# Regrouping the small matmuls of a gated recurrence and of windowed attention inside a two-layer mixer kernel

## The chip, the cores and the metric

The kernel runs on one core of one Trainium2 chip. The metric is the device time of one execution in microseconds. A core has five engines that run side by side and wait for one another through semaphores: TensorE (PE in the profile, its weight loads shown apart as PEld), VectorE (DVE), ScalarE (ACT), GpSimd (POOL, nearly unused here) and SyncE (SP), which issues most of the DMAs.

## What is computed

Two layers (DEPTH = 2) of one mixer run over 640 tokens of width 2048: 128 context tokens and 512 latent ones. In each layer a normalised and modulated x is multiplied by one input matrix of 6656 columns, whose columns feed three branches side by side; their outputs are concatenated, multiplied by one output matrix, gated and added to x. The two branches that the change touches are these (cut from the reference):

```
def sink_attend(qb, keys, vals, mask, sink):          # 8 query heads, 2 kv heads, blocks of 128 queries
    s = jnp.einsum('bhgqd,bhkd->bhgqk', qb, keys) * (HEAD_DIM ** -0.5)
    ...
    p = jnp.exp(s - m)
    denom = jnp.sum(p, axis=-1, keepdims=True) + jnp.exp(sk - m)
    out = jnp.einsum('bhgqk,bhkd->bhgqd', p / denom, vals)

def hgrn_scan(q, k, v, logf, s0):                     # 4 heads, both directions, chunks of 32 tokens
    def step(S, xs):
        b = jnp.cumsum(lfc, axis=-2)
        qe = qc * jnp.exp(b)
        ke = kc * jnp.exp(-b)
        att = jnp.where(causal, jnp.einsum('bhtd,bhsd->bhts', qe, ke), 0.0)
        o = jnp.einsum('bhtd,bhdv->bhtv', qe, S) + jnp.einsum('bhts,bhsv->bhtv', att, vc)
        S = jnp.exp(b_last)[..., 0, :, None] * S + jnp.einsum('bhsd,bhsv->bhdv', kc * jnp.exp(b_last - b), vc)
```

## The kernel before

**The big products.** Tokens stand as five tiles of 128. Each weight tile of 256 KB is loaded by SP (`wraw`, L662), split into a rounded part `wh` on ACT (L670) and a remainder `wl` on DVE (L671), and each product is made of three matmuls (`wh` with the rounded activations `hh`, `wl` with `hh`, `wh` with the remainder `hl`). `rowmajor` gives 512 columns for five token tiles (L682, L683, L684, 128x512 each); `colmajor` gives 128 columns for all tokens (L690, a 128x384 and a 128x256 matmul for each of the three). All of this work runs through `self.pm`, five PSUM banks named m.

**The small work.** Attention, the recurrence and the gating branch are generators in a list, `self.side`. `rowmajor` and `colmajor` call `tick()` every few matmuls, which runs the first generator to its next `yield`; so small instructions are written down between big ones. They use three PSUM banks named s (`bank()`). A further generator, `ada_gen`, computes modulation vectors on DVE from weights that SP loads (L311, `aacc<-wa,s,aacc`).

**What sets the order.** The program is recorded through a scheduling layer. It keeps data dependencies, and from the written order and its own idea of times it lays down a fixed sequence for each engine. At run time each engine works through its sequence strictly in order, and an instruction whose inputs are late holds up all that stands behind it on that engine. `keep_in_program_order(x)` adds one rule: x may not be placed ahead of the instruction that was written before it on its engine. It does not forbid that others are placed between.

**Attention** (`attn`, 20 calls: two layers, two kv heads, one context tile t = 0 and four latent tiles). The scores of four heads are made, masked and exponentiated on ACT (L955); DVE forms the reciprocal of the denominator (L958); ACT multiplies each head's row by it (L960, four ACTIVATEs). Then for each block of 128 keys: four transposes through TensorE, one per head, into one s bank (L971); ACT copies the bank into a rounded part (L974), DVE forms the remainder (L975), and three 128x512 matmuls add into the output bank: L983 with the rounded part, L984 with the remainder, L985 with the rounded part again. There are 56 such latent key blocks, and four for the context tile.

**The recurrence** (`hgrn`, 8 calls: two layers, four heads). After the states are made, the five token tiles are gone through as steps n. In a step `build(n)` writes the decayed keys of each direction d into a buffer `K[d]` of which there is one (7 ACT copies per direction, L1120 and L1124). Four matmuls per direction with 32 output columns each (L1138) give a 128x128 block of scores in a bank of its own; DVE masks it into `att[d]` (L1141), and adds both directions (L1143). One step later TensorE transposes the sum (L1161), ACT copies it (L1163, `aT`), and two steps after that three matmuls (L1150, two L1153) give the tile's output, which ACT squares and copies (L1156, L1157).

## Times and profile before

| | us |
|---|---|
| median of 3 runs | 2282.91 (2281.86 to 2283.32) |
| the profiled execution | 2287.63 |
| its span, first to last instruction | 2285.8 |
| PE busy in the span | 2242.6 (13259 matmuls) |
| DVE / ACT busy | 1381.1 / 943.9 |
| transposes L971 | 240, 45.6 busy |
| score matmuls L1138 | 640 records, 33.7 busy |

The profile shows one execution. Busy times of PE overlap, since the next matmul starts while the one before drains; what a matmul costs is therefore read from the distance between starts. A matmul on unrounded 32-bit numbers stands in the trace as two records, so 320 matmuls of L1138 are 640 records. In a timeline row the columns are the start in us, the length in us, engine, line, operation, output and inputs, shapes, the number of merged instructions, and in brackets the idle time of the engine before them with what ended it. PEld rows are weight loads; one that had to wait shows idle time there even where PE itself still drains older work.

### The profile page before, as it was taken

The numbers are of one execution on the slowest core, as the hardware profiler recorded it, in microseconds if no ns is written. First come the engines' busy times: TensorE is split into PE (matmuls) and PEld (weight loads), VectorE is DVE, ScalarE is ACT, GpSimd is POOL, SyncE is SP. The second block draws the span as 40 slices with busy tenths as digits, with TensorE's granted clock in tenths as the row PEclk, the third lists the DMA queues.
The fourth block names the chain that finished last, engine by engine and source line by source line (L and its number), as shares of the span: only waits on it lengthen the run. The fifth ranks groups of instructions, "written<-read, shape, count | busy, mean of one in ns | idle before, by whom it ended". The sixth has DMA issues, their size and how long they took to land.

```text
span 2285.8 us, 35095 instructions
## 1 busy us (share of the span) xinstructions
PE 2242.6 (98%) x13259; PEld 1945.6 (85%) x13259; DVE 1381.1 (60%) x2666; ACT 943.9 (41%) x2306; POOL 0.7 (0%) x8
## 2 busy tenths in 40 slices
PE   7999999999999999999989999999999999999999
PEld 4766778999999998978877887799999999898887
DVE  4457967748577575776668555844846644264332
ACT  3423355445464562422223345543635545233111
POOL 0000000000000000000000000000000000000000
PEclk9999999999999999999999999999999999999999
DMA  9776533324334254465553321422423322326332
GB/s 354 243 258 209 171 95 117 117 78 145 103 114 133 83 154 129 144 224 182 177 181 94 101 61 48 131 60 82 140 76 103 111 69 82 94 70 205 113 106 79
DMA packets 265550, 299.03 MB, mean 131 GB/s; under 512 B 16771, under 2 KB 166165, under 8 KB 263845
## 3 DMA queue, kind: packets, MB, share of 16 engines
q1 hardware_dynamic: 252656, 270.09, 37.9%
q10 hardware_dynamic: 12724, 26.71, 3.7%
q8 instruction: 104, 1.70, 0.3%
q14 instruction: 66, 0.53, 0.1%
HBM read 281.69 MB, written 15.04 MB: 130 GB/s over the span
## 4 chain that ended last, share of the span: by engine, by line
PE 87%; DVE 6%; DMA 5%; ACT 1%; issue 1%; ACTq 0%; SPq 0%; DVEq 0%
PE m L690 36%; PE m L682 12%; PE m L684 12%; PE m L683 12%; DMA wa<-in_w_ada_dram 4%; DVE aacc L311 2%; PE s L249 2%; PE s L925 2%; PE s L971 1%; PE s L1138 1%; DVE wl L671 1%; PE s L983 1%; PE s L690 1%; PE s L984 1%; PE s L1153 1%
## 5 line engine op out<-in xcount | busy, mean ns | idle before, releaser
L671 DVE TENSOR_TENSOR wl<-wr,wh 128x512 fp32r<-128x512 f32 (+1 forms) x535 | 366.5, 687 | 547.5 <-ACT wh L670 546.5
L670 ACT ACTIVATE wh<-wr 128x512 fp32r<-128x512 f32 (+1 forms) x535 | 335.9, 629 | 870.6 <-PE m L684 501.7
L683 PE MATMUL m<-wl,hh 128*128 128x512 f32 x1440 | 568.1, 395 | 5.9 <-DVE wl L671 5.7
L682 PE MATMUL m<-wh,hh 128*128 128x512 f32 x1440 | 571.0, 397 | 1.6 <-ACT hh L396 1.5
L684 PE MATMUL m<-wh,hl 128*128 128x512 f32 x1440 | 566.1, 393 | 0.0
L690 PE MATMUL m<-hh,wh 128*128 128x384 f32 x2016 | 479.1, 317 | 0.2 <-DVE ev L1189 0.2
L690 PE MATMUL m<-hh,wl 128*128 128x384 f32 x2016 | 468.1, 311 | 0.0
L690 PE MATMUL m<-hl,wh 128*128 128x384 f32 x2016 | 467.3, 311 | 0.0
L311 DVE SCALAR_TENSOR_TENSOR aacc<-wa,s,aacc 128x512 f32<-128x512 f32 x480 | 344.1, 746 | 84.9 <-DMA wa<-in_w_ada_dram 82.7
L682 PEld LDWEIGHTS m<-wh,hh 128*128 128x128 f32 x1440 | 271.9, 189 | 73.8 <-issue 9.8
L683 PEld LDWEIGHTS m<-wl,hh 128*128 128x128 f32 x1440 | 272.0, 189 | 65.7 <-DVE wl L671 9.6
L690 PEld LDWEIGHTS m<-hh,wh 128*128 128x128 f32 x2016 | 310.8, 189 | 14.7 <-issue 9.3
L684 PEld LDWEIGHTS m<-wh,hl 128*128 128x128 f32 x1440 | 271.8, 189 | 58.5 <-issue 2.4
L690 PEld LDWEIGHTS m<-hh,wl 128*128 128x128 f32 x2016 | 311.5, 189 | 2.0 <-issue 1.8
L690 PEld LDWEIGHTS m<-hl,wh 128*128 128x128 f32 x2016 | 311.2, 189 | 2.0 <-issue 1.4
L1124 ACT ACTIVATE mg<-ev,Dt 128x32 f32<-128x32 f32 x480 | 113.3, 309 | 10.3 <-PE s L1138 10.1
L955 ACT ACTIVATE g<-g,st,qs 128x384 f32<-128x384 f32 (+1 forms) x64 | 48.1, 752 | 31.6 <-DVE st L951 31.6
L975 DVE TENSOR_TENSOR g<-s,g 128x512 fp32r<-128x512 f32 x56 | 38.6, 690 | 36.3 <-ACT g L974 29.2
L971 PE MATMUL s<-misc,g 128*128 128x128 f32 x240 | 45.6, 284 | 5.9 <-ACT g L960 5.1
L960 ACT ACTIVATE g<-g,st 128x384 f32<-128x384 f32 (+2 forms) x80 | 43.9, 605 | 13.3 <-DVE st L958 13.3
L925 PE MATMUL s<-kT,g 128*128 128x256 f32 (+1 forms) x288 | 47.3, 305 | 0.0
L971 PEld LDWEIGHTS s<-misc,g 128*128 128x128 f32 x240 | 29.6, 142 | 20.1 <-ACT g L960 12.3
(278 smaller groups left out, 1832.4 us busy)
## 6 DMA issues: line engine op xcount, KB each, us to landing
wr<-in_w_in_dram SPq DMA_DIRECT2D x406, 256.0 KB, 2.9
wa<-in_w_ada_dram SPq DMA_DIRECT2D x296, 256.0 KB, 2.9
wr<-in_w_out_dram SPq DMA_DIRECT2D x128, 256.0 KB, 3.0
wa<-in_w_ada_dram SPq DMA_DIRECT2D x16, 1024.0 KB, 7.0
wa<-in_w_in_dram SPq DMA_DIRECT2D x9, 1024.0 KB, 6.4
mg<-in_w_ada_dram SPq DMA_DIRECT2D x4, 1280.0 KB
x<-mg SPq DMA_DIRECT2D x20, 256.0 KB, 2.6
mg<-x ACTq DMA_DIRECT2D x5, 1024.0 KB, 6.1
```

The source lines that it names most:

```text
L249: return self.nc.tensor.matmul(acc[32 * q:32 * q + 32, 0:n], lhsT=lhs[:, kk, :], rhs=rhs, start=kk < 4, stop=kk >= 12, skip_group_check=True)
L311: nc.vector.scalar_tensor_tensor(acc[:, cd], r, sc, acc[:, cd], op0=ALU.mult, op1=ALU.add)
L670: nc.scalar.activation(wh, raw, AF.Copy)
L671: nc.vector.tensor_tensor(wl, raw, wh.bitcast(F32), op=ALU.subtract)
L682: nc.tensor.matmul(ps, lhsT=hh, rhs=wh[:, 0], start=k == 0, stop=False)
L683: nc.tensor.matmul(ps, lhsT=hh, rhs=wl[:, 0], start=False, stop=False)
L684: nc.tensor.matmul(ps, lhsT=hl, rhs=wh[:, 0], start=False, stop=k == KT - 1)
L690: self.nc.tensor.matmul(ps[hf][:, 0:n], lhsT=w[:, a], rhs=h[:, o:o + n], start=k == 0 and i == 0, stop=k == KT - 1 and i == 2)
L925: nc.tensor.matmul(so, lhsT=x[:, hs], rhs=y[:, ks], start=i == 0, stop=i == 2, skip_group_check=True)
L955: nc.scalar.activation(dst[h], src[h], AF.Exp, bias=nmx[:, h:h + 1], scale=rq[:, h:h + 1], accum_out=den[:, h:h + 1])
L971: nc.tensor.transpose(pb[:, h * P:(h + 1) * P], dst[h][:, kb * P:(kb + 1) * P], self.ident)
L1124: nc.scalar.activation(blk[:, 4 * i + q], e[:, q], AF.Copy, scale=dd[:, i, c:c + 1])
```

## The change

Four things are edited, and nothing of the arithmetic but one order of addition.

- In `attn`, the scaling by the reciprocal denominator is shared: heads 0 and 2 go to DVE (`tensor_scalar`), heads 1 and 3 stay on ACT.
- In the same function the loop over key blocks first writes the three value matmuls of the block before, and then the four transposes of this block. The value matmul with the remainder comes first of the three. The transposes go from head 3 down to head 0. The instructions of such a group, all but its first, are tied with `keep_in_program_order`.
- In `hgrn`, both directions' scores go into one bank, and are masked by one DVE operation of 256 columns; for that `att` becomes one tile of two halves, and the mask constant swaps its halves.
- In a step n of `hgrn` these are now written in one row and tied: the eight score matmuls of tile n, the transpose of tile n-1, and the three output matmuls of tile n-2. Transpose and output share one bank `y`. The copies on DVE and ACT and `build(n + 1)` are written behind them. A head has seven steps with two yields each (before: eight steps and 13 yields).

```
--- before.py
+++ after.py
@@ -69,7 +69,7 @@
     for cd in range(2):
         misc[cd::32, 248 + cd] = 1.0
     c["misc"] = misc
-    c["tri"] = np.stack([q <= k, q >= k], axis=1).astype(np.float32)
+    c["tri"] = np.stack([q >= k, q <= k], axis=1).astype(np.float32)
     return c
 
 
@@ -218,11 +218,11 @@
             mf = self.g(512)
             nc.scalar.dma_start(mf, C["mask"][:, 512 * i:512 * i + 512])
             nc.vector.tensor_copy(self.mask[:, 512 * i:512 * i + 512], mf)
-        self.att = [cst.tile([P, P], F32, name=f"att{d}") for d in range(2)]
+        self.att = cst.tile([P, 2, P], F32, name="att")
         self.tp = [cst.tile([P, 5, 5], F32, name=f"tp{i}") for i in range(2)]
         for d in range(2):
             nc.gpsimd.memset(self.tp[d], 0.0)
-            nc.gpsimd.memset(self.att[d], 0.0)
+            nc.gpsimd.memset(self.att[:, d], 0.0)
         self.snk = cst.tile([P, 2, 8], F32, name="snk")
         self.nsnk = cst.tile([P, 2, 8], F32, name="nsnk")
         nc.scalar.dma_start(self.snk, I["attn_sink"].partition_broadcast(P))
@@ -957,18 +957,33 @@
         nc.vector.tensor_tensor(den, den, es, op=ALU.add)
         nc.vector.reciprocal(den, den)
         for h in range(4):
-            nc.scalar.activation(dst[h], dst[h], AF.Copy, scale=den[:, h:h + 1])
+            if h % 2:
+                nc.scalar.activation(dst[h], dst[h], AF.Copy, scale=den[:, h:h + 1])
+            else:
+                nc.vector.tensor_scalar(dst[h], dst[h], den[:, h:h + 1], None, op0=ALU.mult)
         yield
         yield
         yield
         yield
         o = self.bank()
         pend = None
+        keep = self.tc.keep_in_program_order
         for kb in range(nb + 1):
+            if kb > 0:
+                first, last = kb == 1, kb == nb
+                if t > 0:
+                    v = [self.vT[:, gi, i, vb[kb - 1]] for i in range(2)]
+                    nc.tensor.matmul(o, lhsT=v[0], rhs=pend[1], start=first, stop=False)
+                    keep(nc.tensor.matmul(o, lhsT=v[0], rhs=pend[0], start=False, stop=False))
+                    keep(nc.tensor.matmul(o, lhsT=v[1], rhs=pend[0], start=False, stop=last))
+                else:
+                    nc.tensor.matmul(o, lhsT=self.vprm(gi), rhs=pend, start=first, stop=last)
             if kb < nb:
                 pb = self.bank()
-                for h in range(4):
-                    nc.tensor.transpose(pb[:, h * P:(h + 1) * P], dst[h][:, kb * P:(kb + 1) * P], self.ident)
+                for h in range(3, -1, -1):
+                    x = nc.tensor.transpose(pb[:, h * P:(h + 1) * P], dst[h][:, kb * P:(kb + 1) * P], self.ident)
+                    if kb or h < 3:
+                        keep(x)
                 if t > 0:
                     pt = (self.g(512, F32R), self.g(512, F32R))
                     nc.scalar.activation(pt[0], pb, AF.Copy)
@@ -976,15 +991,6 @@
                 else:
                     pt = self.g(512)
                     nc.scalar.activation(pt, pb, AF.Copy)
-            if kb > 0:
-                first, last = kb == 1, kb == nb
-                if t > 0:
-                    v = [self.vT[:, gi, i, vb[kb - 1]] for i in range(2)]
-                    nc.tensor.matmul(o, lhsT=v[0], rhs=pend[0], start=first, stop=False)
-                    nc.tensor.matmul(o, lhsT=v[0], rhs=pend[1], start=False, stop=False)
-                    nc.tensor.matmul(o, lhsT=v[1], rhs=pend[0], start=False, stop=last)
-                else:
-                    nc.tensor.matmul(o, lhsT=self.vprm(gi), rhs=pend, start=first, stop=last)
             pend = pt
             yield
         nc.scalar.activation(A, o, AF.Copy)
@@ -1128,41 +1134,55 @@
         K = build(0)
         yield
         aTs, sums = {}, {}
-        for n in range(NT + 3):
+        both = lambda a: a.rearrange("p d k -> p (d k)")
+        keep = self.tc.keep_in_program_order
+        for n in range(NT + 2):
             if n < NT:
+                ab = self.bank()
                 for d in range(2):
                     qe = pre[d][1]
-                    ab = self.bank()
                     for i in range(4):
                         ri = 3 - i if d else i
-                        nc.tensor.matmul(ab[32 * i:32 * i + 32, 0:P], lhsT=qe[:, n * P + 32 * i:n * P + 32 * i + 32],
+                        x = nc.tensor.matmul(ab[32 * i:32 * i + 32, d * P:(d + 1) * P],
+                                         lhsT=qe[:, n * P + 32 * i:n * P + 32 * i + 32],
                                          rhs=K[d][:, ri * P:(ri + 1) * P], start=True, stop=True,
                                          skip_group_check=True)
-                    nc.vector.copy_predicated(self.att[d], self.m8[:, 1 - d], ab[:, 0:P])
-                asum = self.sml.tile([P, P], F32, tag="asum", name=self.nm("asum"), bufs=2)
-                nc.vector.tensor_tensor(asum, self.att[0], self.att[1], op=ALU.add)
-                sums[n] = asum
-                if n + 1 < NT:
-                    K = build(n + 1)
-            if n >= 3:
-                j = n - 3
-                oo = self.bank()
-                nc.tensor.matmul(oo[:, 0:P], lhsT=aTs[j], rhs=vj[j], start=True, stop=j == 0)
+                        if d or i:
+                            keep(x)
+            if n > 0:
+                y = self.bank()
+            if 1 <= n <= NT:
+                x = nc.tensor.transpose(y[:, 0:P], sums.pop(n - 1), self.ident)
+                if n < NT:
+                    keep(x)
+            if n >= 2:
+                j = n - 2
+                oo = y[:, P:2 * P]
+                x = nc.tensor.matmul(oo, lhsT=aTs[j], rhs=vj[j], start=True, stop=j == 0, skip_group_check=True)
+                if n <= NT:
+                    keep(x)
                 if j > 0:
                     for d in range(2):
-                        nc.tensor.matmul(oo[:, 0:P], lhsT=pre[d][2][:, j * P:(j + 1) * P],
-                                         rhs=S[d][:, order[d].index(j) - 1], start=False, stop=d == 1)
+                        keep(nc.tensor.matmul(oo, lhsT=pre[d][2][:, j * P:(j + 1) * P],
+                                              rhs=S[d][:, order[d].index(j) - 1], start=False, stop=d == 1,
+                                              skip_group_check=True))
+            if n < NT:
+                nc.vector.copy_predicated(both(self.att), both(self.m8), ab[:, 0:2 * P])
+                asum = self.sml.tile([P, P], F32, tag="asum", name=self.nm("asum"), bufs=2)
+                nc.vector.tensor_tensor(asum, self.att[:, 0], self.att[:, 1], op=ALU.add)
+                sums[n] = asum
+            if 1 <= n <= NT:
+                aT = self.sml.tile([P, P], F32, tag="aT", name=self.nm("aT"), bufs=2)
+                nc.scalar.activation(aT, y[:, 0:P], AF.Copy)
+                aTs[n - 1] = aT
+            if n >= 2:
                 junk = self.sml.tile([P, P], BF16, tag="junk", name=self.nm("junk"), bufs=1)
-                nc.scalar.activation(junk, oo[:, 0:P], AF.Square, accum_out=ss[:, j:j + 1])
-                nc.scalar.activation(ob[:, j * P:(j + 1) * P], oo[:, 0:P], AF.Copy)
+                nc.scalar.activation(junk, oo, AF.Square, accum_out=ss[:, j:j + 1])
+                nc.scalar.activation(ob[:, j * P:(j + 1) * P], oo, AF.Copy)
+            if n + 1 < NT:
+                K = build(n + 1)
             yield
-            if 1 <= n <= NT:
-                tb = self.bank()
-                nc.tensor.transpose(tb[:, 0:P], sums.pop(n - 1), self.ident)
-                aT = self.sml.tile([P, P], F32, tag="aT", name=self.nm("aT"), bufs=2)
-                nc.scalar.activation(aT, tb[:, 0:P], AF.Copy)
-                aTs[n - 1] = aT
-                yield
+            yield
         nc.scalar.activation(ss, ss, AF.Ln, bias=self.bias[:, 0:1], scale=1.0 / P)
         nc.scalar.activation(ss, ss, AF.Exp, scale=-0.5)
         for j in range(NT):
```

**What this moves on TensorE in the recurrence.** First the place in layer 0, head 0, at step 1 of 5, before the change. L1138 are the score matmuls of one direction (`g_4966` forward, `g_5158` backward), L1161 the transpose; L690 are big column products.

```order
L1138 MATMUL s_5444<-mg_4962,g_4966 32x128 x4
L690 MATMUL m_5300<-hh_688,wh_5434 128x384
...
L690 MATMUL m_5300<-hl_718,wh_5434 128x384
L1138 MATMUL s_5450<-mg_4962,g_5158 32x128 x4
L690 MATMUL m_5301<-hl_718,wh_5434 128x256
L690 MATMUL m_5300<-hh_717,wl_5432 128x384
L690 MATMUL m_5301<-hh_717,wl_5432 128x256
L1161 MATMUL s_5484<-misc,asum_5406 128x128
```

The same place after the change; L1146 are the score matmuls, L1155 the transpose, L1161 now the first output matmul.

```order
L690 MATMUL m_5300<-hh_717,wl_5432 128x256
L1146 MATMUL s_5453<-mg_4961,g_4965 32x128 x4
L1146 MATMUL s_5453<-mg_4961,g_5157 32x128 x4
L1155 MATMUL s_5462<-misc,asum_5403 128x128
L690 MATMUL m_5299<-hh_746,wh_5431 128x384
```

Nine and then three big matmuls stood between the parts; now none does. Over the whole program 64 groups of four score matmuls stood by themselves before and 8 steps had all eight together; now 26 groups of four and 27 steps with eight. In 13 of the 40 steps the two directions are still apart, three big matmuls between them.

**What it moves on TensorE in attention.** Layer 0, a latent tile, the first key blocks, before the change. L971 are transposes (the second name is the head's row), L983 to L985 the value matmuls, L682 to L684 big row products.

```order
L971 MATMUL s_2527<-misc,g_2455 128x128
L971 MATMUL s_2549<-misc,g_2455 128x128
L684 MATMUL m_2404<-wh_2855,hl_689 128x512
L971 MATMUL s_2527<-misc,g_2461 128x128
...
L983 MATMUL s_2526<-g_2532,vT_1633 128x512
L684 MATMUL m_2402<-wh_2912,hl_718 128x512
L682 MATMUL m_2403<-wh_2912,hh_717 128x512
L984 MATMUL s_2526<-g_2533,vT_1633 128x512
L985 MATMUL s_2526<-g_2532,vT_1633 128x512
L971 MATMUL s_2567<-misc,g_2455 128x128
```

The same place after; L984 are now the transposes, L976 the value matmul with the remainder, L977 and L978 those with the rounded part.

```order
L984 MATMUL s_2526<-misc,g_2454 128x128
L684 MATMUL m_2403<-wh_2854,hl_689 128x512
...
L684 MATMUL m_2400<-wh_2911,hl_718 128x512
L976 MATMUL s_2525<-g_2532,vT_1632 128x512
L977 MATMUL s_2525<-g_2531,vT_1632 128x512
L978 MATMUL s_2525<-g_2531,vT_1632 128x512
L984 MATMUL s_2551<-misc,g_2478 128x128
```

Before, the transposes came in twos as each head's row became ready, and L983 stood apart from L984. Now a key block is one group of seven, headed by the matmul that needs the remainder from DVE. Between the last transpose of a block and that matmul stand seven row matmuls here; over the program the big work at that place is seven matmuls 512 wide or ten of 384 and 256 in 40 of the 56 cases, and more in the others.

**What it moves on ACT in the recurrence.** After the change, the build of the keys for step 3 in layer 0, head 0: L1126 and L1130 are the copies into `K` (`ev_4431` forward, `ev_4633` backward), L1176 is `aT`, L1180 and L1181 square and copy the output, L670 is a weight split, L1014 the evacuation of a big product.

```order
L1126 ACTIVATE mg_4961<-ev_4431 128x4x32
L1130 ACTIVATE mg_4961<-ev_4431,Dt_4975 128x32 x2
L1176 ACTIVATE aT_5532<-s_5526 128x128
L1180 ACTIVATE junk_5534,oss_5366<-s_5526 128x128
L1181 ACTIVATE g_5365<-s_5526 128x128
L670 ACTIVATE wh_5695<-wr_5693 128x512
L1014 ACTIVATE ev_5561<-m_5299 128x384
L1014 ACTIVATE ev_5561<-m_5300 128x256
L1130 ACTIVATE mg_4961<-ev_4431,Dt_4975 128x32 x3
L1126 ACTIVATE mg_4961<-ev_4633 128x4x32
L1130 ACTIVATE mg_4961<-ev_4633,Dt_5167 128x32 x6
```

The copy of the transposed sum and the two reads of the output bank now stand in the middle of the build, so that the rest of the build is behind them on ACT.

## Prediction

> **What bounds the kernel now.** I read the page's busy times first, then its chain of waits, and then the timeline of TensorE at the places that the change moves.
>
> ```profile
> PE 2242.6 (98%) x13259; PEld 1945.6 (85%) x13259; DVE 1381.1 (60%) x2666; ACT 943.9 (41%) x2306; POOL 0.7 (0%) x8
> PE 87%; DVE 6%; DMA 5%; ACT 1%; issue 1%; ACTq 0%; SPq 0%; DVEq 0%
> ```
>
> TensorE is busy for 98% of the span and carries 87% of the chain that ended last. So a change is worth what it takes out of TensorE's own sequence: matmuls that cost more than their streaming, and waits in the midst. Work moved on DVE or ACT counts only where TensorE waits for it. The number of big matmuls is not changed, nor is the number of small ones.
>
> **Term 1: eight score matmuls instead of twice four.** The first four rows show four score matmuls (eight records) between big column products, the row ahead of them a plain pair; the last four rows, from an earlier place, show all eight together.
>
> ```profile
> 569.08 0.46 PE L690 MATMUL m<-hl,wh 128*128 128x384 f32 x2
> 569.37 0.45 PE L690 MATMUL m<-hh,wl 128*128 128x384 f32 x2
> 569.76 0.43 PE L1138 MATMUL s<-mg,g 128*32 128x128 f32 x8
> 570.11 0.56 PE L690 MATMUL m<-hh,wh 128*128 128x384 f32 x2
> 570.51 0.46 PE L690 MATMUL m<-hl,wh 128*128 128x384 f32 x2
> ...
> 562.04 0.45 PE L690 MATMUL m<-hh,wl 128*128 128x384 f32 x2
> 562.42 0.64 PE L1138 MATMUL s<-mg,g 128*32 128x128 f32 x16
> 563.00 0.56 PE L690 MATMUL m<-hh,wh 128*128 128x384 f32 x2
> 563.39 0.46 PE L690 MATMUL m<-hl,wh 128*128 128x384 f32 x2
> ```
>
> A pair of 384 and 256 columns takes 569.37 - 569.08 = 0.29. With four score matmuls inside, two pairs take 570.51 - 569.37 = 1.14 instead of 0.58, so a group of four costs 0.56. With eight they take 563.39 - 562.04 = 1.35, so a group of eight costs 0.77. Two groups merged save 2 x 0.56 - 0.77 = 0.35. The sequence has 64 groups of four before and 26 after: 19 merges, 19 x 0.35 = 6.7 us. Bounds: none of it, if the merged group meets a wait at its fifth matmul; and 6.7 plus the idle time that PE has at these matmuls now:
>
> ```profile
> L1138 PE MATMUL s<-mg,g 128*32 128x128 f32 x640 | 33.7, 287 | 2.6 <-DVE mg L1109 2.4 <-ACT mg L1124 0.2
> ```
>
> 2.6 us, nearly all of it one wait for the state update, which this change does not touch. I take 6.7.
>
> What a boundary costs can be seen on the weight loads at the lone group:
>
> ```profile
> 569.75 0.16 PEld L1138 LDWEIGHTS s<-mg,g 128*32 128x32 f32 x8 [0.19 <-ACT mg L1124]
> 570.11 0.30 PEld L690 LDWEIGHTS m<-hh,wh 128*128 128x128 f32 x2 [0.20 <-issue]
> ```
>
> The loader stands idle for 0.19 ahead of the group and 0.20 behind it: at these boundaries loads are not brought forward under the running matmul. The Trainium skill, "TensorE: Matmul & The Clock Gate", section "LDWEIGHTS (loading the stationary operand)", prices a load at its columns divided by 1.2 per ns; exposing one load of 32 and one of 128 columns per removed boundary would make term 1 an estimated 19 x 0.13 = 2.5 us. The trace does not agree: its idle times there, 0.19 and 0.20, are both longer than that.
>
> **Term 2: the transpose and the output matmuls of the recurrence join the group.** The output matmuls now stand behind a group in some steps:
>
> ```profile
> 580.87 0.49 PE L1150 MATMUL s<-mg,aT 128*128 128x128 f32 x2
> 581.20 0.61 PE L1153 MATMUL s<-mg,g 128*128 128x128 f32 x4
> 581.56 0.36 PE L690 MATMUL m<-hl,wh 128*128 128x256 f32 x1
> ```
>
> Six records in 581.56 - 580.87 = 0.69, 0.115 each, their streaming alone. A transpose costs 0.12 (below). Neither is dearer alone, so joining them saves nothing: 0.
>
> The other side is the build of the keys on ACT, which must fit between two groups, since there is one buffer per direction:
>
> ```profile
> 564.89 0.29 ACT L1120 ACTIVATE mg<-ev 128x128 f32<-128x128 f32 x1
> 566.36 0.29 ACT L1120 ACTIVATE mg<-ev 128x128 f32<-128x128 f32 x1
> 567.84 0.29 ACT L1120 ACTIVATE mg<-ev 128x128 f32<-128x128 f32 x1
> 568.69 0.63 ACT L670 ACTIVATE wh<-wr 128x512 fp32r<-128x512 f32 x1 [0.56 <-PE m L690]
> 570.50 0.26 ACT L1163 ACTIVATE aT<-s 128x128 f32<-128x128 f32 x1
> ```
>
> One direction takes 1.47, both 567.84 - 564.89 = 2.95. In the new sequence 24 big column matmuls (12 x 0.29 = 3.48) stand between most groups, and the rest of the group itself (0.2 of scores, 0.12, six times 0.115) adds up to 1.0: some 4.5 for ACT's 2.95 plus one split (0.63), `aT` (0.26) and the start behind TensorE. In the step whose build also holds the two reads of the output bank (0.3 each, as the nearest row, `aT`, has it) and an evacuation (two like the split, 1.3), ACT has 5.7; there the sequence has the directions apart, by three more big matmuls, but little or nothing is left over. I charge 0.1 on each of the 8 such steps: 1 us lost. It is the first rival if it is more.
>
> **Term 3: attention's waits.** These rows, from the lists of what an engine sat idle for, are for the transposes (L971), L983 and L984, in that order:
>
> ```profile
>   ACT g L960: 17.4, 31
> ...
>   ACT g L974: 4.3, 17
> ...
>   DVE g L975: 4.3, 21
> ```
>
> 26.0 us in 69 waits. That is idle time of TensorE or of its weight loader, and not all of it is lost. A key block as it runs now shows how much:
>
> ```profile
> 306.35 0.40 PE L683 MATMUL m<-wl,hh 128*128 128x512 f32 x1
> 306.58 0.38 PE L971 MATMUL s<-misc,g 128*128 128x128 f32 x2
> 306.89 1.09 ACT L974 ACTIVATE g<-s 128x512 fp32r<-128x512 f32 x2 [0.54 <-PE s L971]
> 307.04 0.39 PE L682 MATMUL m<-wh,hh 128*128 128x512 f32 x1
> 307.27 0.40 PE L683 MATMUL m<-wl,hh 128*128 128x512 f32 x1
> 307.52 0.69 DVE L975 TENSOR_TENSOR g<-s,g 128x512 fp32r<-128x512 f32 x1 [0.95 <-ACT g L974]
> 307.54 0.50 PE L983 MATMUL s<-g,vT 128*128 128x512 f32 x1
> 307.54 0.19 PEld L983 LDWEIGHTS s<-g,vT 128*128 128x128 f32 x1 [0.31 <-ACT g L974]
> 307.88 0.40 PE L684 MATMUL m<-wh,hl 128*128 128x512 f32 x1
> 308.27 0.19 PEld L984 LDWEIGHTS s<-g,vT 128*128 128x128 f32 x1 [0.19 <-DVE g L975]
> 308.36 0.42 PE L984 MATMUL s<-g,vT 128*128 128x512 f32 x1
> ```
>
> A 512-column matmul takes 307.27 - 307.04 = 0.23. Two transposes and two such matmuls take 307.04 - 306.35 = 0.69, so a transpose costs 0.12. Around L983 two starts are 307.88 - 307.27 = 0.61 apart instead of 0.46: 0.15 lost where the loader was idle for 0.31. Some 0.15 per wait is thus covered, and the 69 waits cost 26.0 - 69 x 0.15 = 15.6 us now.
>
> After the change each of the 56 latent key blocks has one group headed by the remainder's matmul, and each of the 20 calls one first group of transposes. The chain to the head is the same: the last transpose started near 306.7, DVE ends at 308.21, the load can go at 308.27, 1.57 later. The sequence leaves the transpose's 0.12 and seven 0.23 (1.73) or ten column matmuls (five 0.29, 1.57) at 40 of 56 places. So the head meets its data with 0 to 0.15 to spare if ACT and DVE are free; I charge 0.1 for a just-late load, 5.6 us for 56. At the first groups four ACT scalings become two on ACT and two on DVE, side by side:
>
> ```profile
> L960 ACT ACTIVATE g<-g,st x80: 385/610/726, 289.1 to 1531.1; 128x384 f32<-128x384 f32 x32, 128x512 f32<-128x512 f32 x32, 128x128 f32<-128x128 f32 x16
> ```
>
> 0.61 each, so ACT's part shrinks from 2.4 to 1.2, but TensorE now needs head 3 first, which is ready about when head 1 was. A wait there costs 17.4 / 31 - 0.15 = 0.41 now; I take half for 20 groups, 4 us. Together 9.6 after against 15.6: 6 us saved. Bounds: all 15.6 saved; or, if each head stands behind one more DVE operation half of the time (0.69 / 2 = 0.35 on 56), 19.6 lost, 13.6 beyond the forecast.
>
> **What costs nothing.** Forty scalings go to DVE. The nearest row is the 0.69 of a two-input operation over 512, so 40 x 0.69 = 28 us at the most, in two stretches (columns: time, PE, PEld, DVE, ACT busy, as in the stages view):
>
> ```profile
> 280.00:500.00 220.00, 215.19 (x1300) 191.00 (x1300) 148.32 (x324) 112.20 (x243) 0.00 (x0) 0.99 0.35 105
> 1320.00:1540.00 220.00, 218.82 (x1173) 183.09 (x1172) 133.46 (x303) 114.14 (x246) 0.00 (x0) 1.00 0.25 75
> ```
>
> DVE has 72 and 87 us free there, under TensorE's products; without that cover it would be those 28 us. The one mask operation instead of two, and the extra yield of a head, have the same cover. SP's and POOL's queues are not moved past anything.
>
> **Sum.** Against the profiled execution's own 2287.63 (span 2285.8): -6.7 + 0 + 1 - 6 = -11.7, so 2275.9. The median of the runs is 2282.91, 4.7 below that execution; the same difference gives 2271.2.
>
> **Rivals.** Of this kernel a measurement can tell about 0.2%, 4.6 us, from no change.
>
> Only the merging shows. The waits of attention change places (from L960 and L974 to DVE's L975) and cost the same: -6.7 + 1 = -5.7, 2277. For it: DVE works strictly in order, and the remainder heads every group. Against it: 69 waits become 76, but 1.57 us of chain are mostly covered.
>
> All of attention's waits vanish as well, since each group waits once, for the last input of the group: -6.7 - 15.6 = -22.3, 2260.6. For it: the sequence leaves about the length of the chain. Against it: only about.
>
> Nothing is left over: DVE's queue delays the heads as in the lower bound, but at a third of it (0.11 more on 56, 6 us on top), and term 3 is 0: with some loss in the builds, -6.7 + 4 = -2.7, 2280.
>
> Slower: the build of the keys becomes the bound of the recurrence. `aT` stands inside the build, and behind it on ACT stands the build's rest. It reads the bank which the output matmuls still write; if ACT has to hold there until the group ends, about 1.2 us behind the first four, and nothing of the build ran before, ACT needs 1.2 + 2.95 + 0.63 + 0.26 + 0.6 = 5.6 in a period of 3.48 + 1.5 = 5.0: 0.6 on each of 32 builds, 19 us lost, +19 - 6.7 - 6 = +6, 2289. It decides from 0.4 per build (13 us eat terms 1 and 3). The Trainium skill, "PSUM — Partial Sum Buffer", section "PSUM bank collisions raise a hardware error", says that engines must be kept apart by whole banks, which would hold ACT there in just this way. Against the rival: three or four copies of the build stand ahead of `aT` in ACT's sequence, and the idle time of L1138 is now small.
>
> That the change doesn't do what it says holds in part: 13 of 40 steps stay apart, which is in term 1.
>
> **How the numbers follow.** Forecast 0.52, only the merging 0.19, all waits gone 0.11, nothing left 0.10, slower 0.08. The first three are faster by more than 4.6 us, but a few us of waits elsewhere can shift with a new sequence, so I take 0.79 faster, 0.13 the same, 0.08 slower. The range goes from just under the case of all waits gone to that of nothing left, 2258 to 2282. The forecast by itself would reach from 2265 to 2277.
>
> **What would show it.** Term 1: in the changed kernel, two pairs of column products with eight score matmuls take 1.35, and a group of seven or eleven records has no idle loader inside. Term 2: PE's idle time at the score matmuls stays under some 4 us. Term 3: the waits before the transposes fall from 17.4 to well under 10, and those at the head of the value matmuls, all for DVE's remainder, stay under 10. The forecast is wrong if waits for the key copies or for the remainder reach 20 us, or if waits that no term names, such as those for `wl`, move by more than the terms.

## The result

| | us |
|---|---|
| changed kernel, median of 4 runs | 2269.61 (2269.33 to 2270.33) |
| kernel before, median of 4 runs | 2283.11 (2281.86 to 2283.86) |
| ratio | 0.9937 (95% interval 0.9925 to 0.9949) |
| the profiled execution after, its span | 2269.36, 2267.6 |
| PE, DVE, ACT busy in it | 2229.4, 1388.6, 921.2 |

Faster by 14 us; the forecast was 2271.2. The total came out, and that is luck: the recurrence gave twice what was charged to it, attention about a third, and the two errors nearly cancel. The rest of this section shows where; the experiments then separate the halves.

The busy times and the chain of waits of the changed kernel, from its page:

```profile
PE 2229.4 (98%) x13259; PEld 1942.3 (86%) x13259; DVE 1388.6 (61%) x2666; ACT 921.2 (41%) x2266; POOL 0.7 (0%) x8
PE 85%; DMA 6%; DVE 6%; ACT 1%; issue 1%; ACTq 0%; SPq 0%; DVEq 0%
```

The number of matmuls is the same and TensorE still carries the chain. The 14 us came out of its own sequence.

**The recurrence.** Two steps of one call, TensorE's timeline of the changed kernel (L1146 scores, L1155 transpose, L1161 and L1166 outputs). In the first step the scheduler left four scores apart, in the second all eight stand together with the rest:

```profile
569.74 0.46 PE L690 MATMUL m<-hh,wl 128*128 128x384 f32 x2
570.13 0.42 PE L1146 MATMUL s<-mg,g 128*32 128x128 f32 x8
570.49 0.56 PE L690 MATMUL m<-hh,wh 128*128 128x384 f32 x2
570.88 0.34 PE L690 MATMUL m<-hl,wh 128*128 128x384 f32 x1
571.15 0.43 PE L1146 MATMUL s<-mg,g 128*32 128x128 f32 x8
571.51 0.33 PE L1155 MATMUL s<-misc,asum 128*128 128x128 f32 x1
571.68 0.39 PE L1161 MATMUL s<-mg,aT 128*128 128x128 f32 x2
571.90 0.61 PE L1166 MATMUL s<-mg,g 128*128 128x128 f32 x4
572.26 0.36 PE L690 MATMUL m<-hl,wh 128*128 128x256 f32 x1
572.47 0.45 PE L690 MATMUL m<-hh,wl 128*128 128x384 f32 x2
...
575.11 0.46 PE L690 MATMUL m<-hh,wl 128*128 128x384 f32 x2
575.50 0.64 PE L1146 MATMUL s<-mg,g 128*32 128x128 f32 x16
576.07 0.33 PE L1155 MATMUL s<-misc,asum 128*128 128x128 f32 x1
576.24 0.39 PE L1161 MATMUL s<-mg,aT 128*128 128x128 f32 x2
576.46 0.61 PE L1166 MATMUL s<-mg,g 128*128 128x128 f32 x4
576.83 0.54 PE L690 MATMUL m<-hh,wh 128*128 128x384 f32 x2
577.20 0.45 PE L690 MATMUL m<-hl,wh 128*128 128x384 f32 x2
```

The first step costs (570.88 - 569.74) - 0.58 = 0.56 for the lone four, and (572.47 - 570.88) - 0.29 = 1.30 for four with the transpose and the outputs: 1.86. The second costs (577.20 - 575.11) - 0.58 = 1.51. So a merge is worth 0.35, as the prediction had it.

The loader's rows (PEld) of the second step, and the last key copies ahead of it on ACT:

```profile
574.82 0.53 ACT L1130 ACTIVATE mg<-ev,Dt 128x32 f32<-128x32 f32 x2
575.50 0.38 PEld L1146 LDWEIGHTS s<-mg,g 128*32 128x32 f32 x16 [0.20 <-ACT mg L1130]
576.07 0.14 PEld L1155 LDWEIGHTS s<-misc,asum 128*128 128x128 f32 x1 [0.20 <-issue]
576.07 0.36 PEld L1161 LDWEIGHTS s<-mg,aT 128*128 128x128 f32 x2
576.35 0.53 PEld L1166 LDWEIGHTS s<-mg,g 128*128 128x128 f32 x4
576.80 0.30 PEld L690 LDWEIGHTS m<-hh,wh 128*128 128x128 f32 x2
```

The loader is idle for 0.20 ahead of the first 32-column load and 0.20 ahead of the first 128-column load behind the scores, here the transpose's. From the outputs to the big product it isn't idle at all. What costs is the switch between the two widths of load, not the border between small and big work.

**All places together.** From the starts of the matmuls in a trace, from the first big product on, one can work out what TensorE spends beyond streaming the big products: each interval between two starts, less 0.227 where it begins with a 512-column big matmul and 0.175 or 0.117 for one of 384 or 256 columns (0.29 a pair), put down to the recurrence or to attention by the small matmuls that stand there (a group that holds any matmul of attention counts there whole). Before: recurrence 102.9, attention 144.9, all else 137.1, sum 384.9. After: 90.5, 140.2, 135.8, sum 366.5. (The first two expectations below quote 12.7 and 7.7 for these differences; that count took intervals between two groups with a single big matmul between them twice. Counted once they are 12.4 and 4.7.)

Sorted by what stands in a group, nearly all groups of one kind cost the same in the changed kernel: a lone four 0.552 at the least, a lone eight 0.770, four with transpose and outputs 1.286, eight with them 1.504; the transpose alone 0.112, output matmuls alone 0.670. The recurrence's 12.4 are then:

- 19 merges at 2 x 0.552 - 0.770 = 0.334 each: 6.4;
- the transpose behind scores: 0.112 alone, 0.067 behind eight scores (0.837 less 0.770), and 0.552 + 0.112 + 0.670 = 1.334 for four scores, transpose and outputs apart, 1.286 together; over the 32 transposes that now stand there some 1.5;
- waits, that is, costs above the least of the same kind: 5.4 at scores, transposes and outputs before, 0.7 after: 4.7 (the state matmuls, L1109, lose 0.2 of it again).

One place alone holds 3.9 of the 5.4 before. Rows of DVE and TensorE there, in the kernel before:

```profile
737.45 1.42 DVE L311 SCALAR_TENSOR_TENSOR aacc<-wa,s,aacc 128x512 f32<-128x512 f32 x2 [0.89 <-DMA wa<-in_w_ada_dram]
738.78 0.72 DVE L1109 SCALAR_TENSOR_TENSOR mg<-mg,EG,s 128x128 f32<-128x128 f32 x2
740.02 0.34 DVE L1109 SCALAR_TENSOR_TENSOR mg<-mg,EG,s 128x128 f32<-128x128 f32 x1
740.51 0.66 PE L1138 MATMUL s<-mg,g 128*32 128x128 f32 x8 [2.43 <-DVE mg L1109]
```

The DVE stands still for the DMA of `wa`, works off `aacc`, and only then comes to the state update for which a lone four of scores on TensorE waits 2.4 us. Behind this wait the granted clock is half, as a row of the stages view shows (the third number from the right):

```profile
741.00:746.00 5.00, 5.00 (x27) 4.19 (x24) 2.99 (x8) 3.43 (x14) 0.00 (x0) 0.50 0.40 117
```

A pair of column products takes 0.53 there instead of 0.29. The trace has the clock at 0.50 from 740.2 to 747.0, which costs another 1.4 at the recurrence's groups and some 1.5 at the big products between them. The other two traces with the recurrence of before, attention only and scalings only below, have the same wait (2.6 and 2.3) and 3.4 us at half clock behind it.

The scores read nothing that the state update writes. By the code, what they lack is a bank: the small work has three, the two directions of the step before hold one each until DVE masks them, and the update still reads the third. With one bank for both directions this wait is gone: in all three traces with two banks the scores wait for the update once, in none of the ten with one. In the changed kernel DVE stands for the same DMA and has the same `aacc` ahead of the update (L1115), but no score matmul waits for it:

```profile
731.23 1.42 DVE L311 SCALAR_TENSOR_TENSOR aacc<-wa,s,aacc 128x512 f32<-128x512 f32 x2 [1.96 <-DMA wa<-in_w_ada_dram]
732.56 1.11 DVE L1115 SCALAR_TENSOR_TENSOR mg<-mg,EG,s 128x128 f32<-128x128 f32 x3
733.70 0.42 PE L1146 MATMUL s<-mg,g 128*32 128x128 f32 x8
```

**Attention.** From the lists of what the engine sat idle for in the changed kernel, the rows of the transposes (L984) and of the first value matmul (L976), in that order:

```profile
  ACT g L961: 9.2, 23
...
  DVE g L990: 10.5, 43
```

The waits fell from 26.0 in 69 to 19.7 in 66. At the groups that hold nothing but transposes and value matmuls, 147 before and 70 after, the time beyond their own streaming fell from 17.7 to 11.0. Where value matmuls now stand ahead of a next call's scores, 2.0 came back.

### The profile page after: what moved, and what is told of

Same layout as the page of the kernel before. It is cut to its first block, busy times and chain, and to the rows that moved or that the text cites. A ratio compares the mean times of both kernels' runs of the same rounds, so it can differ in the third digit from the quotient of the medians.

```text
span 2267.6 us, 34992 instructions
## 1 busy us (share of the span) xinstructions
PE 2229.4 (98%) x13259; PEld 1942.3 (86%) x13259; DVE 1388.6 (61%) x2666; ACT 921.2 (41%) x2266; POOL 0.7 (0%) x8
## 4 chain that ended last, share of the span: by engine, by line
PE 85%; DMA 6%; DVE 6%; ACT 1%; issue 1%; ACTq 0%; SPq 0%; DVEq 0%
PE m L690 36%; PE m L682 12%; PE m L684 12%; PE m L683 12%; DMA wa<-in_w_ada_dram 5%; DVE aacc L311 2%; PE s L249 2%; PE s L925 2%; PE s L984 1%; DVE wl L671 1%; PE s L1146 1%; PE s L976 1%; PE s L1109 1%; PE s L1166 1%; PE s L690 1%
## 5 line engine op out<-in xcount | busy, mean ns | idle before, releaser
L670 ACT ACTIVATE wh<-wr 128x512 fp32r<-128x512 f32 (+1 forms) x535 | 335.7, 628 | 833.8 <-PE m L684 493.6
L682 PE MATMUL m<-wh,hh 128*128 128x512 f32 x1440 | 570.2, 396 | 1.6 <-ACT hh L396 1.5
L684 PE MATMUL m<-wh,hl 128*128 128x512 f32 x1440 | 565.6, 393 | 0.0
L690 PE MATMUL m<-hh,wh 128*128 128x384 f32 x2016 | 473.5, 314 | 0.0
L690 PE MATMUL m<-hl,wh 128*128 128x384 f32 x2016 | 465.2, 310 | 0.0
L690 PE MATMUL m<-hh,wl 128*128 128x384 f32 x2016 | 461.2, 309 | 0.0
L682 PEld LDWEIGHTS m<-wh,hh 128*128 128x128 f32 x1440 | 271.8, 189 | 73.9 <-issue 9.3
L684 PEld LDWEIGHTS m<-wh,hl 128*128 128x128 f32 x1440 | 271.7, 189 | 59.7 <-issue 3.8
L690 PEld LDWEIGHTS m<-hh,wh 128*128 128x128 f32 x2016 | 309.7, 188 | 9.4 <-issue 5.0
L690 PEld LDWEIGHTS m<-hl,wh 128*128 128x128 f32 x2016 | 309.7, 188 | 0.0
L690 PEld LDWEIGHTS m<-hh,wl 128*128 128x128 f32 x2016 | 308.4, 188 | 0.0
L1130 ACT ACTIVATE mg<-ev,Dt 128x32 f32<-128x32 f32 x480 | 115.9, 314 | 22.9 <-PE s L1146 22.7
L989 ACT ACTIVATE g<-s 128x512 fp32r<-128x512 f32 x56 | 33.5, 598 | 72.2 <-PE s L984 72.1
L1170 DVE COPY_PREDICATED att<-m,s 128x256 f32<-128x256 uint8 x40 | 17.9, 447 | 51.4 <-PE s L1146 51.4
L929 DVE CUSTOM_DVE_ANT_0 g<-s,mask 128x384 f32<-128x384 f32 (+1 forms) x64 | 38.2, 622 | 11.3 <-PE s L925 11.1
```

The lines of the kernel that those rows point to most:

```text
L670: nc.scalar.activation(wh, raw, AF.Copy)
L682: nc.tensor.matmul(ps, lhsT=hh, rhs=wh[:, 0], start=k == 0, stop=False)
L684: nc.tensor.matmul(ps, lhsT=hl, rhs=wh[:, 0], start=False, stop=k == KT - 1)
L690: self.nc.tensor.matmul(ps[hf][:, 0:n], lhsT=w[:, a], rhs=h[:, o:o + n], start=k == 0 and i == 0, stop=k == KT - 1 and i == 2)
L1130: nc.scalar.activation(blk[:, 4 * i + q], e[:, q], AF.Copy, scale=dd[:, i, c:c + 1])
```

## The experiments

All compare with runs of the kernel before on the same chip; its median was 2282.5 to 2284.8 in these sets. The columns on the right are TensorE's time beyond the big products, from one profiled execution each, so that 1 or 2 us there mean little: three traces with the attention of before read 144.9, 142.9 and 143.8. In the two runs with scalings only, fewer matmuls of `ada_gen` stand in attention's groups; by the lines of the matmuls their advantage over the change at attention's places is 1 to 2 us, not 2 to 3.

| run | median us | ratio to before (95%) | recurrence | attention | all else |
|---|---|---|---|---|---|
| kernel before | | 1 | 102.9 | 144.9 | 137.1 |
| the change | 2269.61 | 0.9937 (0.9925 to 0.9949) | 90.5 | 140.2 | 135.8 |
| the change, again | 2269.24 | 0.9938 (0.9926 to 0.9951) | 90.5 | 140.7 | 135.0 |
| recurrence only | 2271.65 | 0.9953 (0.9940 to 0.9965) | 91.0 | 142.9 | 134.4 |
| attention only | 2281.79 | 0.9993 (0.9985 to 1.0002) | 102.4 | 140.7 | 137.0 |
| no ties | 2268.36 | 0.9933 (0.9919 to 0.9946) | 90.3 | 138.2 | 137.0 |
| scores in one bank, alone | 2280.60 | 0.9986 (0.9977 to 0.9995) | 98.9 | 143.8 | 136.1 |
| backward scores first | 2266.85 | 0.9926 (0.9913 to 0.9938) | 86.7 | 141.0 | 137.0 |
| the same, attention untied | 2264.07 | 0.9916 (0.9903 to 0.9928) | 87.2 | 139.7 | 136.7 |
| scalings only | 2278.27 | 0.9978 (0.9969 to 0.9987) | 102.3 | 137.8 | 138.9 |
| backward first, scalings only | 2264.14 | 0.9914 (0.9901 to 0.9928) | 87.1 | 137.9 | 137.1 |
| copies on ACT added | 2280.74 | 0.9992 (0.9982 to 1.0001) | 101.0 | 140.6 | 136.8 |
| longer key builds | 2284.37 | 0.9998 (0.9987 to 1.0009) | 105.5 | 140.2 | 137.7 |

### The two halves

The first run has the change's `hgrn` with the `attn` of before; the second the change's `attn` with the `hgrn` of before. Each is the diff of the change with the other function's part left out.

> The change's recurrence (merged and tied scores, the transpose and output matmuls in the group), with the attention of before. The order has 27 groups of eight score matmuls and 26 of four, as the changed kernel. The prediction's terms 1 and 2 give -5.7 us against the kernel before (19 merges x 0.35, less 1 for the builds), so about 2277.4. What the two traces show at the places of the recurrence gives more: time of TensorE beyond the streaming of the big products fell there by 12.7 us, so 2270 to 2273 if it was not the one profiled execution of before that was slow there. Third theory, nothing comes from the recurrence and it was attention's waits: 2282 to 2284.

> The change's attention (scalings shared by DVE and ACT, value matmuls of the block before ahead of the transposes, remainder first, ties), with the recurrence of before. Term 3 gives -6 us: about 2277. The two traces' difference at these places is -7.7: 2275.5. If the waits only change places: 2282 to 2284. If all waits of attention vanish: -15.6, 2267.5. If the gains of the two halves add, this run's and the other half's differences from the kernel before sum to about -14.

The recurrence alone takes 2283.89 - 2271.65 = 12.2 us, attention alone 2.1, and its interval reaches past 1. Together 14.3, the change's 13.5 to 14.2: the halves add up, and they are 12 and 2, not 5.7 and 6. The whole of the change that can be told from no change is in the recurrence.

### Scores in one bank, alone

In the kernel before, both directions' scores go to one bank, are tied, and are masked together; transposes and outputs stay where they were.

```diff
         for n in range(NT + 3):
             if n < NT:
+                ab = self.bank()
                 for d in range(2):
-                    ab = self.bank()
...
-                    nc.vector.copy_predicated(self.att[d], self.m8[:, 1 - d], ab[:, 0:P])
...
+                nc.vector.copy_predicated(both(self.att), both(self.m8), ab[:, 0:2 * P])
```

> The kernel before with one edit: the scores of both directions go to one bank, tied, with one mask operation; the transposes and output matmuls stay where they were, each step with its two yields, and so does attention. The order merges little: 14 groups of eight and 52 of four (8 and 64 before). By the price of term 1 alone 64 x 0.56 + 8 x 0.77 less 52 x 0.56 + 14 x 0.77 = 2.1 us less: 2281, no change that can be told. If the merged group must wait for the later of the two key builds and the builds stand behind a mask that is now later, it is slower, 2284 to 2290. If the bank and the mask were the gain of the recurrence, it would come near the run with the whole recurrence.

Measured 3.3 us faster, 4.0 at the recurrence's places. Few groups merge (67 separate runs of scores in the trace instead of 72, 1.7 at 0.334 each), and the waits above the least price, with those of the state matmuls, fell from 8.0 to 5.8. Most of that is the wait for the state update. In these rows a lone four of scores starts at 738.41, while the update, behind the same DMA and `aacc`, ends only at 739.17 + 0.34:

```profile
736.60 1.42 DVE L311 SCALAR_TENSOR_TENSOR aacc<-wa,s,aacc 128x512 f32<-128x512 f32 x2 [2.06 <-DMA wa<-in_w_ada_dram]
737.93 0.73 DVE L1109 SCALAR_TENSOR_TENSOR mg<-mg,EG,s 128x128 f32<-128x128 f32 x2
738.41 0.43 PE L1138 MATMUL s<-mg,g 128*32 128x128 f32 x8
739.17 0.34 DVE L1109 SCALAR_TENSOR_TENSOR mg<-mg,EG,s 128x128 f32<-128x128 f32 x1
```

So the shared bank and mask are a part of the gain, not all of it; the other 8 us come with the groups that the joined step allows.

### No ties

```diff
-        keep = self.tc.keep_in_program_order
+        keep = lambda x: x
```

in both functions; nothing else.

> The changed kernel without its ties: the scheduler orders the small matmuls freely; the code's order of calls, the shared bank and the shared scalings stay. The order then has 35 groups of eight score matmuls and 10 of four (27 and 26 with ties), but some steps have the eight in two parts with the transpose and outputs between, and the waits of attention are met anywhere in a block. If only the number of score groups sets the gain, 35 x 0.77 + 10 x 0.56 against 27 x 0.77 + 26 x 0.56 is 2.8 us less: about 2267 (the change: 2269.6). If the ties themselves bring something (one wait per burst, the transpose and outputs at a group's end), it is slower than the change, 2271 to 2276.

Neither slower, as the one theory had it, nor 2.8 faster: 2268.36, not to be told from the change. The recurrence has the same 53 runs of scores. Eight of its steps are torn in a new way, as this piece of TensorE's timeline of the untied kernel shows:

```profile
1912.08 0.46 PE L690 MATMUL m<-hh,wl 128*128 128x384 f32 x2
1912.46 0.43 PE L1146 MATMUL s<-mg,g 128*32 128x128 f32 x8
1912.82 0.33 PE L1155 MATMUL s<-misc,asum 128*128 128x128 f32 x1
1912.99 0.39 PE L1161 MATMUL s<-mg,aT 128*128 128x128 f32 x2
1913.21 0.39 PE L1166 MATMUL s<-mg,g 128*128 128x128 f32 x2
1913.53 0.42 PE L1146 MATMUL s<-mg,g 128*32 128x128 f32 x8
1913.88 0.49 PE L1166 MATMUL s<-mg,g 128*128 128x128 f32 x2
1914.13 0.54 PE L690 MATMUL m<-hh,wh 128*128 128x384 f32 x2
1914.51 0.45 PE L690 MATMUL m<-hl,wh 128*128 128x384 f32 x2
```

All eight scores are inside one stretch of small work, and yet it costs (1914.51 - 1912.08) - 0.58 = 1.85, the price of a step in two groups (1.86), not 1.51. That is what settles the switch against the border: no big matmul stands between, but the loads change width four times. In attention the ties bring nothing: 138.2 without them here and 139.7 in a later run, 140.2 to 141.0 with them.

### Backward scores first, and attention untied

```diff
-                for d in range(2):
+                for d in (1, 0):
...
-                        if d or i:
+                        if not d or i:
                             keep(x)
```

A group's first wait is then for the key build that ends last, and the order has all 40 steps in one group. The second run also takes attention's ties away; the third has this recurrence with the attention of before but for the two scalings.

> The changed kernel with one edit: in a step the four score matmuls of the backward direction are issued ahead of the forward ones, so that the group's first wait is for the key build that is finished last. In the order all 40 steps then have their eight together (27 in the changed kernel). The prices read from the changed kernel's trace (a group of four 0.55, eight 0.77, four with transpose and outputs 1.29, eight with them 1.50) make the recurrence's bursts 57.0 us instead of 62.0: 5 less, about 2264.6 (the change: 2269.6). Rival: the second build is late in just those 13 steps, which is why the scheduler had split them; TensorE then waits for it at the group's head. A wait of 0.4 on each of 13 eats the gain: 2269 to 2271, with the wait shown at the score matmuls for ACT's key build (6.8 us in the changed kernel, 12 or more then).

> As the run before it (backward scores first), and attention without its ties, so that the scheduler places transposes and value matmuls as it likes; the recurrence keeps its ties. The run without any ties had 2 us less at attention's places than the changed kernel (138.2 against 140.2 of TensorE's time beyond the big products) and all of its loss in the recurrence (eight steps where an output pair was torn from its group, 1.84 instead of 1.50). By that: 2262 to 2263. If attention's ties are worth something: 2266 or more. If free ties change nothing: as the run before it.

> The recurrence with the backward scores first (all 40 steps have eight together), and attention as it was before the change but for the two scalings on DVE: no ties and no moved value matmuls in attention. If the moved matmuls and ties of attention gave nothing, this is as fast as the run with attention untied, 2262 to 2265, and faster than the run with backward first and the change's attention (2266.9). If the moved value matmuls gave something that only the ties took back, it is 2266 or more.

> The changed kernel itself, on the chip of the run above and against the same runs of the kernel before, so that the two can be set side by side: 2269 to 2271, ratio 0.993 to 0.995. The run above is 5 to 7 us below it if the prices of the groups (5 us less) and the ties of attention (2 to 3 us) add up, less the waits that the merged groups meet (1 us in the two runs with the backward scores first).

Backward first gives 2266.85, 2.8 under the change's median, where 5.0 were expected; the two ratios, 0.9926 and 0.9937, overlap in their intervals, so the time alone doesn't tell it from no difference. At its places the recurrence fell from 90.5 to 86.7, 3.8. The waits for ACT, from the scores' idle list of this run, are 7.4, against 6.8 in the changed kernel, not the 12 of the rival:

```profile
  ACT mg L1130: 7.4, 28
```

The 1.2 that are missing at the places are waits in two kinds of group (1.0 and 0.4 above their least). The 1.0 is one group, which waits for the last key copy of its step:

```profile
743.47 0.65 PE L1146 MATMUL s<-mg,g 128*32 128x128 f32 x16 [0.91 <-ACT mg L1130]
```

The other two runs have the same wait there, 1.5 and 1.0: what the rival said of 13 steps came true in one. Untying attention takes off another 2.8, as expected, but these two intervals overlap as well. The third run, side by side with the change, is 2264.14 (2262.94 to 2265.31) against 2269.24 (2267.47 to 2271.18): 5.1 us faster than the change and 19 faster than the kernel before. It and the untied version are alike.

### Scalings only

```diff
-            nc.scalar.activation(dst[h], dst[h], AF.Copy, scale=den[:, h:h + 1])
+            if h % 2:
+                nc.scalar.activation(dst[h], dst[h], AF.Copy, scale=den[:, h:h + 1])
+            else:
+                nc.vector.tensor_scalar(dst[h], dst[h], den[:, h:h + 1], None, op0=ALU.mult)
```

> The kernel before with one edit: two of the four scalings of a call go to DVE. The order of the matmuls, the ties and the recurrence are as before. The transposes at the head of a call lost 10 to 12 us beyond their streaming before, and 5.0 in the changed kernel; if that is the scaling, this run is 5 us faster than the kernel before, about 2279, and the moved matmuls and ties of attention gave nothing or cost 2 to 3 (the whole attention part: 2281.8). If the first groups gained from the reversed order of the heads and the ties, this run is the same as before, 2283 to 2284.

4.2 us faster (interval 0.9969 to 0.9987): more than the whole attention part of the change (2.1). The rows of its transposes that are for the scalings, on DVE and on ACT (17.4 in 31 before), and then of the value matmul that waits for the remainder:

```profile
  DVE g L963: 2.3, 6
...
  ACT g L961: 0.6, 2
...
  DVE g L978: 3.4, 16
```

The wait for the scalings is nearly gone. The remainder is waited for 16 times instead of the change's 43; the matmul with the rounded part goes first, and has waits of its own:

```profile
  ACT g L977: 4.2, 15
```

Together these are 7.6 in 31, against 10.5 in 43. So what the change moved in attention beside the scalings, the order, the remainder ahead and the ties, cost it about 2 us. The intervals of this run and of attention only still overlap (up to 0.9987, and from 0.9985); the two runs above that give up the ties, or ties and order, point the same way.

### More work on ACT

To see how near the key builds are to being the bound, copies were added to ACT: first four small ones per build that write a tile which nothing reads, then, in the last run, two of the build's own copies twice.

```diff
                 e, dd = c4(pre[d][0])[:, j], pre[d][3][:, j]
+                for _ in range(4):
+                    nc.scalar.activation(self.extra, e[:, 0], AF.Copy)
```

```diff
-                        nc.scalar.activation(blk[:, 4 * i + q], e[:, q], AF.Copy, scale=dd[:, i, c:c + 1])
+                        for _ in range(3 if i == 1 else 1):
+                            nc.scalar.activation(blk[:, 4 * i + q], e[:, q], AF.Copy, scale=dd[:, i, c:c + 1])
```

> The changed kernel with four additional copies of 128x32 on ACT in each direction's key build, 8 x 0.21 = 1.7 us more per pair of builds; they write a tile that nothing reads. 32 builds stand between two score groups. By the prediction's account of a step (4.5 us between groups against 2.95 of builds, 0.63 of a split and 0.26 of the copy, 0.66 to spare) some 1.0 us is uncovered on each of 24 to 32 builds: 25 to 33 us slower than the change, 2295 to 2303, with the waits of the score matmuls for ACT at 30 us or more. If ACT's chain has 1.7 us to spare in a step (the builds start earlier than that account says), nothing changes: 2269 to 2272. If ACT was the bound already in all 32: 32 x 1.7 = 54 us, 2324.

> The changed kernel with two of the key copies of each direction's build repeated, 4 x 0.21 = 0.85 us more of ACT in each step; the repeated copies write the same values to the same place, so that they cannot be moved out of the step as the added copies of an earlier run were. The scheduler knows of them and puts the score matmuls otherwise: 87 separate runs of score matmuls in the order instead of 53. If what a run of score matmuls costs is its two switches of the loader (0.33 for each run more, as the step from twice four to eight shows), the 34 more cost 11 us: 2280 to 2282. If TensorE also waits for the longer builds (0.85 less the 0.3 that the second build has to spare in the changed kernel, on 32 steps), 18 more: about 2298, with waits of the score matmuls for ACT that grow by as much. If builds and score groups are both free, 2269 to 2271.

The first of the two doesn't answer its question. It is 11 us slower, but the added copies depend on nothing in the step, and the scheduler ran them far ahead, as these rows of ACT and TensorE show:

```profile
652.86 2.58 ACT L1128 ACTIVATE extra<-ev 128x32 f32<-128x32 f32 x10
655.34 0.58 ACT L1106 ACTIVATE g<-s 128x512 f32<-128x512 f32 x1
...
655.97 1.16 PE L1110 MATMUL s<-mg,g 128*128 128x128 f32 x8 [2.48 <-ACT g L1106]
```

Ten of them stand in front of the copy of the transposed keys, for which the state matmuls wait. The 11 us are there (10.3 at these matmuls by the starts), and the steps saw none of it.

The second kept its copies inside the step: 15 us slower than the change, 2284.37. The scheduler tore the groups into 87 runs of scores, and 105.5 - 90.5 = 15.0 is what the recurrence lost at its places. The costs above the least of their kind, with those of the state matmuls, are 4.2 in all, against 3.5 in the change. So some 14 of the 15 are prices of more runs, 34 at about 0.42, and about 1 is waits: near the first theory's 11, far from the second's 29. A run is dearer than expected since even a single score matmul between big ones costs 0.53 and two 0.54, nearly as much as four (0.552). In the changed kernel the room is small all the same: the last key copy of a step ends, at most of the 32 builds, 0.3 to 0.5 before the fifth score matmul starts (above: 574.82 + 0.53 = 575.35, against 575.50 + 0.24). It suffices because the scheduler put the groups there; with 0.85 more it gave up the groups, and TensorE hardly waits.

## Why the prediction was right, and where not

**Term 1, merging: the price was right, and a bound was wrong.** 19 merges at 0.35 were charged as 6.7; by the prices after they brought 6.4. The Trainium skill, "TensorE: Matmul & The Clock Gate", section "LDWEIGHTS (loading the stationary operand)", has columns divided by 1.2 as a load's time in ns, from which the prediction worked out an estimate of 2.5 us for the 19. The runs don't agree, with 6.4. A step in which no big matmul intervenes (1.85) shows that it is the change of width that costs. The step that failed is the sentence on the idle time of the score matmuls, "nearly all of it one wait for the state update, which this change does not touch". The change did touch it: with one bank for both directions the scores need none that the update still reads. And the list of idle times, 2.6, held only half of what was to be had: 1.4 more at the recurrence's groups was the half clock behind that wait, and 1.5 were smaller waits, 0.6 at the most, that the list does not show. 4.7 came from the waits, which no term had, and 1.5 from the transposes. The bound as written, 6.7 plus 2.6, was thus too low for the 12.2 that the recurrence gave.

**Term 2: no loss, and a small gain.** "Joining them saves nothing: 0" was wrong by 1.5: behind scores a transpose adds 0.067 instead of 0.112. The 1 us charged to the builds didn't come; groups of eight in these steps cost 1.505 and 1.056 without exception. The account of a step, 4.5 us for 3.84 of work, was about right: 0.3 to 0.5 to spare.

**Term 3 was too large.** 6 were charged; the halves gave 2.1 by time and about 3 at attention's places (143.9 on average with the attention of before, 140.6 with the change's). By the prediction's own prices the 6 are two parts: 8.7 saved at the first groups (17.4 - 31 x 0.15 = 12.7 before, 4 after), and 2.7 lost at the value matmuls (8.6 - 38 x 0.15 = 2.9 before, 5.6 after). The second was about right, as 2 were lost. The step that failed is the first: the shared scalings alone gave 4.2, half of the 8.7, though the wait for the scalings fell to 2.9 in 8. A wait taken away was worth less than its idle time less 0.15. Part of it came back under other names: waits for anything else in the transposes' list are 6.6 in that run, against 2.3 before. The price of the heads, "0 to 0.15 to spare" and 0.1 for each of 56, was too low as well: the 44 heads in groups of their own cost 0.14 each, and those ahead of a next call's scores, which had no price at all, 2 us together. That the old order covered these better, with the rounded part's matmul between transposes and remainder, fits the shorter list of the run with scalings only, but no run changes the order alone. A bound of this term was also added up wrongly: 0.35 on 56 is 19.6 in place of 5.6, 14.0 beyond the forecast, not 13.6, and a loss of 8.0 against the kernel before, not of 19.6.

**The rivals.** "Only the merging shows" was right on attention, nearly, and wrong on the total, since the recurrence gave the double. "All of attention's waits vanish" and "nothing is left over" are out: 19.7 of waits remain of 26.0, and the change is 14 us faster. The slower one, the key build as the bound, has its mechanism in part: ACT does hold `aT` until the output matmuls have ended.

```profile
577.11 0.28 ACT L1176 ACTIVATE aT<-s 128x128 f32<-128x128 f32 x1 [1.76 <-PE s L1166]
```

The last of them ends at 576.46 + 0.61 = 577.07, while the transpose that `aT` reads ended at 576.40. The Trainium skill, "PSUM — Partial Sum Buffer", section "PSUM bank collisions raise a hardware error", has the rule to guard by bank and quadrant (by bank in its simple version) and not by address. The program's waits are so here: `aT` starts 0.04 after the last matmul into its bank, 0.71 after its own input was there. It costs nothing, because the build's copies stand ahead of `aT`. With 0.85 us more per step the price came, by torn groups and not by waiting.

**What would show it.** Two pairs with eight scores take 1.35 (0.77 and 0.58), as said. That a group has no idle loader inside was wrong: 0.20 between the scores and the transpose. Waits before the transposes, 9.2, are under 10 but not well under; those for the remainder, 10.5, are just over. The waits for `wl` (5.7 before, 6.5 after) stayed.

## What to carry over

Count, in the order of TensorE's matmuls, the places where the width of the weight load changes: each run of narrow matmuls that is merged with its neighbour was worth 0.33 us here, whatever stood between, and the way to merge them is to let the first wait of the run be the one that comes true last. When several edits come together, price the waits by the distance between starts, group by group against the cheapest of the same kind; TensorE's own list of idle times had 2.6 of 5.4 here, and missed the half clock behind a wait above all. Ask of a wait which buffer it is for, and not only which engine ends it: one bank less removed it. And test each edit alone: the ties and the order in attention cost about 2 us here, which the gain of the other edits hid.

## What was not expected of the hardware

The loader's idle time of 0.20 us at each change between 32- and 128-column loads appears in both directions and between small matmuls as well, and a run of one score matmul (0.53) costs nearly as much as a run of four (0.552). Why the loader doesn't go ahead there is not shown by any run, nor whether it is the width itself or something else in which these loads differ.

The clock did not always fall behind a wait. In the trace of before TensorE stood 2.4 us, and 6.8 us at 0.50 followed; in the changed kernel's it stood 2.3 us ahead of 979.25, for `wl`, and the clock stayed at 1.00. When it falls is not shown by these runs.
